# A two-layer hybrid trunk on one core: diagonal blocks through padded matrices, permuted weights in two loads

## The chip, the cores and the metric

The kernel runs on one core of one Trainium2 chip. The metric is the device time of one execution in microseconds. A core has TensorE (PE; matmuls and their weight loads), VectorE (DVE), ScalarE (ACT), GpSimd (POOL) and SyncE (SP), each with its own instruction stream. Nearly all transfers are issued by SP, in order, and carried out by 16 DMA engines.

## The reference

Two layers over 1,024 tokens of width 1,024, in float32. Layer 0 projects the input once and feeds two branches, multiplies each by its own SiLU gate, and projects both out together. Branch A is an RWKV-7 recurrence, 8 heads of 64; branch B is attention of 8 heads over a shared key and value, with the best 256 keys of each query chosen by an indexer. Layer 1 is gated linear attention. Every layer ends in a LayerNorm.

```
def step(S, inp):
    r_t, w_t, k_t, v_t, kk_t, b_t = inp
    sa = jnp.einsum('bhvk,bhk->bhv', S, -kk_t)
    S = S * w_t[:, :, None, :] + sa[..., None] * b_t[:, :, None, :] + v_t[..., None] * k_t[:, :, None, :]
    return S, jnp.einsum('bhvk,bhk->bhv', S, r_t)
...
y = jnp.concatenate([ya, yb], -1).astype(h.dtype) @ e_w_out[j]
```

## The kernel before, in words

The program runs through stages: input projections and indexer scores (to about 170 us), the rest of the projections beside the search for the 256 best keys (to 480), then one mixed stage (to about 815) in which three things run side by side, the last pieces of the output projection with the first LayerNorm (to about 900), and layer 1.

**The mixed stage** holds the attention of eight blocks of 128 queries (`attend`), the recurrence A, and pieces of the output projection. The recurrence is done in 16 chunks of 64 tokens, two chunks to a unit, eight units (`unit`, `chunk`, `finish`). For each of the 8 heads and each chunk a 64x64 triangular matrix must be inverted. `prod` computes the products and `ev_m` stores the matrices as MAB: 128 partitions (two heads' rows of 64) by 8 matrices v by 64 columns. The four 16x16 diagonal blocks of each matrix are inverted first, all 64 lanes at once:

- `f_dm` (L1167) writes the diagonal blocks from MAB to memory, d_m, with eight DMAs of 16 rows each, 8 KB a DMA, in pieces of 64 bytes.
- `f_mt` (L1173) reads them back as Mt, one block to a partition, with two DMAs of 64 rows of 1 KB.
- `f_x` and `f_sub` (L1177, L1185, L1186) run the substitution on POOL: thirty small instructions in a chain.
- `f_dt` (L1191) writes the inverses to memory, d_t, with two DMAs in pieces of 64 bytes.
- `f_tz` (L1195) clears the 128x512 tile TT on POOL, and `f_td` (L1199) reads the diagonal blocks from d_t into TT with eight DMAs.
- `z0` to `e3` (L1226 to L1286) fill in the off-diagonal blocks with small matmuls of 32x32 and 32x16, and `chunk` uses TT in `fu` (L1338).

A chunk needs the state of the chunk before it. MAB has 3 buffers, Mt and Xt 2, TT 3; d_m and d_t take turns among 3.

The order of the stage is written out by hand: each job has an engine, a cost in microseconds, its dependences and the PSUM banks it takes. A loop picks, job by job, the one that can start first by a simple clock for each engine, ties going to the longest remaining chain; for PE a bonus, MODE, favours a job of the same form as the last one (0 plain, 1 chunks and attention values, 2 and 3 the block inverse), and a change of form is charged 0.15 us. The instructions are then pinned to that order on each engine, SP's DMAs among them. So a job's stated cost alters the order of all engines.

**Weights of the output projection**, `e_w_out`, come in tiles of 128 rows by 512 columns (256 KB). For k of 4 and up the rows lie together. For k below 4 they are permuted (two heads of 64 rows each, 128 rows apart), and `rows` gives a view whose outermost size is 2. `wload` (L165), `dealt_weights` (L1555 load, L1560 ACT cast, L92 POOL difference) and `dealt_raw` (L1624) load them into wraw, of which there are three. Pieces of the projection (L1523) take their operands from yt (L1507, L1584, L1512). The attention loads qT by L896 and stores its output by L987.

Of the kernel before, what the change touches and what calls it, by code (L numbers as in the profile page):

```python
# [8 lines left out]
F32 = mybir.dt.float32  # L9
# [12 lines left out]
P = 128  # L22
# [4 lines left out]
CH = 64  # L27
# [11 lines left out]
GTA = (6, 7)  # L39
S = "s"  # L40
BANKS = ("s0", "s1", "s2", "g", "x")
MODE = 5.0
SLIP = 0.15
T0 = 2.0
PEF = 1.0
# [28 lines left out]
def trunk(ctx: ExitStack, tc: tile.TileContext, x, positions, e_w_in, a_mu, a_w0, a_w2, a_a0, a_a2,  # L74
          a_kk_scale, a_ka, a_rk, a_gn_g, a_gn_b, b_kv_norm_g, b_wuk, b_wuv, e_w_out, o_w_in, c_g2,
          c_g_bias, c_norm_g, o_w_out, ln_g, ln_b, out, dbg=None, stop=None):
    nc = tc.nc
    V, A, G, PE = nc.vector, nc.scalar, nc.gpsimd, nc.tensor
# [36 lines left out]
    ewi, ewo, owi, owo = e_w_in[0], e_w_out[0], o_w_in[0], o_w_out[0]  # L115
# [4 lines left out]
    def ct(shape, dt, name):  # L120
        return cp.tile(shape, dt, name=name)
# [40 lines left out]
    def wload(wr, w, c0, n, k, raws=3, bufs=9, scale=None, rows=None, first=None, raw=None):  # L162
        if raw is None:
            raw = (first or wr).tile([P, 512], F32, name="wraw", tag="wraw", bufs=raws)[:, :n]
            nc.sync.dma_start(raw, w[k * P:(k + 1) * P, c0:c0 + n] if rows is None else rows(k, c0, n))  # L165
        hi = wr.tile([P, 512], F32R, name="whi", tag="whi", bufs=bufs)[:, :n]
        lo = wr.tile([P, 512], F32R, name="wlo", tag="wlo", bufs=bufs)[:, :n]
        if scale is None:
            A.copy(hi, raw)  # L169
            gsub(lo, raw, f32(hi))  # L170
        else:
            A.activation(hi, raw, AF.Copy, scale=scale(k))
            V.scalar_tensor_tensor(lo, raw, scale(k), f32(hi), op0=ALU.mult, op1=ALU.subtract)
        return hi, lo
# [57 lines left out]
    d_ya = dram.tile([P, 2, 2, SEQ], F32, name="d_ya")  # L232
    d_yb = dram.tile([4, P, SEQ], F32, name="d_yb")
    d_h1 = dram.tile([SEQ, D], F32, name="d_h1")

# [57 lines left out]
    col, r0 = [], 0  # L295
# [62 lines left out]
    nc.sync.dma_start(wkv[:, 0:CH], b_wuk[0])  # L358
    nc.sync.dma_start(wkv[:, CH:], b_wuv[0])
    ixt = t1.tile([P, NT, N_IX], F32, name="ixt")  # L360
    ssq = ct([P, NT], F32, "ssq")
    sq_scr = t1.tile([P, P], F32, name="sq_scr", tag="cn", bufs=2)
    for t in range(NT):
# [662 lines left out]
    def rt(shape, name, bufs=1, dt=F32, tag=None):  # L1026
        return rw[0 if name in EARLY else 1].tile(shape, dt, name=name, tag=tag or name, bufs=bufs)

    d_m = [dram.tile([8, 8, HB, HB], F32, name=f"d_m{z}") for z in range(3)]
    d_t = [dram.tile([8, 8, HB, HB], F32, name=f"d_t{z}") for z in range(3)]  # L1030
    RUV = {}

    def ruv(c):
# [26 lines left out]
    def unit(u):  # L1060
# [102 lines left out]


        def f_dm(j):
            for g in range(8):
                nc.sync.dma_start(d_m[u % 3][:, g].rearrange("v r t -> r v t"),  # L1167
                                  U["MAB"][g * HB:g * HB + HB, :, g % 4 * HB:g % 4 * HB + HB])

        def f_mt(j):  # L1170
            U["Mt"] = rt([P, HB, HB], "Mt", 2)
            for z in range(2):
                nc.sync.dma_start(U["Mt"][RS[z]].rearrange("l p t -> l (p t)"), d_m[u % 3].rearrange("v b p t -> (v b) (p t)"))  # L1173

        def f_x(j):
            U["Xt"] = rt([P, 8, HB], "Xt", 2)
# [9 lines left out]
            G.tensor_sub(Xt[:, 0:m, jj + 1:], Xt[:, 0:m, jj + 1:], tv)  # L1186

        def f_dt(j):
            dv = d_t[u % 3].rearrange("v b (m z) t -> z (v b) m t", z=2)
            for z in range(2):  # L1190
                nc.sync.dma_start(dv[z], U["Xt"][RS[z]])  # L1191

        def f_tz(j):
            U["TT"] = rt([P, 8, CH], "TT", TB)
            G.memset(U["TT"], 0.0)  # L1195

        def f_td(j):
            for g in range(8):
                nc.sync.dma_start(U["TT"][g * HB:g * HB + HB, :, g % 4 * HB:g % 4 * HB + HB], d_t[u % 3][:, g].rearrange("v r t -> r v t"))  # L1199

        dm = job("S", 4.8, f_dm, mab)
        m_use.append(dm)
        d, use = turn("Mt", 2)
        mt = job("S", 1.2, f_mt, [dm] + d)
# [10 lines left out]
        dt_ = job("S", 1.2, f_dt, [x2_])  # L1215
        use2.append(dt_)
        d, tt_use = turn("TT", TB)
        tz = job("G", 0.6, f_tz, d)
        tt = job("S", 4.8, f_td, [dt_, tz])
        tt_use += [tz, tt]  # L1220
        U["tt_use"] = tt_use


# [261 lines left out]
    wo, operand = [[], []], {}  # L1485
    slots = [0]

    def rows(k, c0, n):

        if k >= 4:  # L1490
            return ewo[k * P:(k + 1) * P, c0:c0 + n]
        m, s = divmod(k, 2)
        return ewo[m * 256:m * 256 + 256, c0:c0 + n].rearrange("(e s d) c -> s e d c", s=2, d=CH)[s]

    def wslot(w, c0, n, k, **kw):

# [53 lines left out]
    def dealt_weights(k):  # L1550
        st = {}

        def f0(j):
            st["raw"] = w0p[0].tile([P, 512], F32, name="wraw", tag="wraw", bufs=3)
            nc.sync.dma_start(st["raw"], rows(k, 0, 512))  # L1555

        def f1(j):
            slots[0] += 1
            wo[0].append([w0p[0].tile([P, 512], F32R, name=x, tag=x, bufs=8) for x in ("whi", "wlo")])
            A.copy(wo[0][k][0], st["raw"])  # L1560

        def f2(j):
            gsub(wo[0][k][1], st["raw"], f32(wo[0][k][0]))

        d, use = turn("wraw", 3)
        a = job("S", 0.6, f0, d, late=WT[0] + WT[1] * k)
        b = job("A", 0.62, f1, [a] + ([(WOJ[-1][0],)] if WOJ else []))
        c = job("G", 1.5, f2, [b])
        use += [a, b, c]
        WOJ.append((b, c))  # L1570
# [50 lines left out]
    def dealt_raw(k):  # L1621
        def f(j):
            RAW1.append(w0p[0].tile([P, 512], F32, name="wraw", tag="wraw", bufs=3))
            nc.sync.dma_start(RAW1[k], rows(k, 512, 512))  # L1624

        d, use = turn("wraw", 3)
        use.append(job("S", 0.6, f, d, late=WT[0] + WT[1] * (NK + 1)))
# [20 lines left out]
    while left:  # L1648
        best = None
        for j in left:  # L1650
            if any(d["start"] is None for d in j["deps"] + j["behind"] + [d for d, _ in j["lag"]]):
                continue
            t = max([clock[j["e"]], j["late"]] + [d["end"] + LAT.get(d["e"], 0.0) for d in j["deps"]]
                    + [d["start"] + 0.001 for d in j["behind"]] + [d["end"] + us for d, us in j["lag"]])
            for names in j["take"]:
                t = max(t, min(held[k] for k in names))
            if t >= 1e9:
                continue
            w = tail[j["n"]] - j["plus"] + (MODE if j["e"] == "PE" and j["mode"] == mode else 0.0)
            key = (round(t / SLIP) * SLIP if j["e"] == "PE" else t, -w)  # L1660
            if best is None or key < best[0]:
                best = key, t, j
        if best is None:
            print([(j["n"], j["e"], j["f"] and j["f"].__code__.co_firstlineno, [d["n"] for d in j["deps"] if d["start"] is None]) for j in left][:60], held)
        _, t, j = best
        j["bank"] = tuple(min(names, key=lambda k: (held[k] > t, names.index(k) if held[k] <= t else held[k])) for names in j["take"])
        us = j["us"]
        if j["e"] == "PE":
            us += 0.15 * (mode != j["mode"])
            mode = j["mode"]  # L1670
        j["start"], j["end"] = t, t + us
        clock[j["e"]] = j["end"]
        for k in j["bank"]:
            held[k] = 2e9
        for g in j["gives"]:
            for k in g["bank"]:
                held[k] = j["end"] + 0.1
        left.remove(j)
        order.append(j)
# [284 lines left out]
```

## Time and profile before

| | |
|---|---|
| runs | 1350.64 us median of 3 (1349.34 to 1355.8) |
| the profiled execution | 1351.04 us, of which the span of the profile is 1349.3 us |
| granted TensorE clock, mean | 0.945 of full speed |
| busy share: PE, PE weight loads, DVE, ACT, POOL | 90%, 71%, 56%, 47%, 31% |
| DMA | 134.77 MB in 170,879 packets, 100 GB/s mean |
| the chain that ended last | PE 52%, DVE 20%, issue 9%, DMA 7%, ACT 6%, POOL 4% of the span |

The page divides the span into 40 slices and gives each engine's share in tenths; the chain that ended last is followed back from the last instruction. An engine's idle time counts only where the work that sets the end waits in it, so the stretches in which TensorE stands still are looked up one by one.

### The profile page before, as it was taken

How to read it: one execution, taken by the hardware profiler on the slowest of the kernel's cores; microseconds unless marked ns; L12 is line 12 of the kernel's file. 1: busy time of each engine (PE TensorE's matmuls, PEld its weight loads, DVE VectorE, ACT ScalarE, POOL GpSimd, SP SyncE). 2: the span in 40 equal slices, each digit the busy share in tenths (PEclk: the TensorE clock that was granted, in tenths of full speed). 3: DMA queues.
4: the chain of work that ended last, by engine and by line, in shares of the span. 5: the costliest groups of instructions: out<-in, count | busy, mean ns of one | idle time of the engine just before them, and what ended most of it. 6: DMA issues, size and time to landing. Idle time of an engine off the chain costs nothing.

```text
span 1349.3 us, 22702 instructions
## 1 busy us (share of the span) xinstructions
PE 1209.7 (90%) x8461; PEld 961.0 (71%) x8461; DVE 752.6 (56%) x1652; ACT 638.0 (47%) x1309; POOL 423.0 (31%) x725
## 2 busy tenths in 40 slices
PE   6998798999988973798999994999999999998997
PEld 5986586676766763586878773877578888887885
DVE  5146879999996542464555532684330114453666
ACT  4247768777722332676677763323651123332100
POOL 3134731444437423443434204212112331142000
PEclk9999899989989986798999996999899999999999
DMA  6102311623425364455554416863102220022321
GB/s 203 32 9 78 107 44 31 164 71 94 125 73 146 113 183 122 124 146 133 148 146 125 115 49 199 273 206 97 32 2 61 63 63 1 1 63 92 119 80 62
DMA packets 170879, 134.77 MB, mean 100 GB/s; under 512 B 62416, under 2 KB 143360, under 8 KB 170768
## 3 DMA queue, kind: packets, MB, share of 16 engines
q1 hardware_dynamic: 167680, 125.87, 32.1%
q10 hardware_dynamic: 3088, 7.44, 1.6%
q8 instruction: 67, 1.10, 0.3%
q14 instruction: 44, 0.36, 0.1%
HBM read 90.27 MB, written 42.99 MB: 99 GB/s over the span
## 4 chain that ended last, share of the span: by engine, by line
PE 52%; DVE 20%; issue 9%; DMA 7%; ACT 6%; POOL 4%; SPq 2%; DVEq 0%; POOLq 0%; ACTq 0%
DVE junk L741 7%; PE op L834 7%; PE s L1523 3%; PE dn L186 3%; PE dn L185 3%; PE dn L184 3%; PE po L979 2%; PE gt L207 2%; PE gt L206 2%; PE gt L208 2%; PE s L956 2%; DMA wraw<-in_e_w_out_dram 2%; POOL wlo L92 1%; PE dn L1860 1%; DMA yt<-d_ya 1%
## 5 line engine op out<-in xcount | busy, mean ns | idle before, releaser
L92 POOL TENSOR_TENSOR wlo<-wraw,whi 128x256 fp32r<-128x256 f32 (+1 forms) x160 | 115.7, 751 | 295.8 <-ACT whi L169 217.4
L184 PE MATMUL dn<-xh,chi 128*128 128x512 f32 x336 | 136.9, 407 | 1.3 <-DVE sg L508 0.7
L186 PE MATMUL dn<-xh,clo 128*128 128x512 f32 x336 | 136.7, 407 | 0.0
L185 PE MATMUL dn<-xl,chi 128*128 128x512 f32 x336 | 135.7, 404 | 0.0
L169 ACT CAST whi<-wraw 128x512 fp32r<-128x512 f32 (+1 forms) x72 | 43.4, 612 | 130.6 <-PE dn L185 65.8
L184 PEld LDWEIGHTS dn<-xh,chi 128*128 128x128 f32 x336 | 65.3, 194 | 22.0 <-issue 7.1
L185 PEld LDWEIGHTS dn<-xl,chi 128*128 128x128 f32 x336 | 65.4, 195 | 18.1 <-issue 4.7
L186 PEld LDWEIGHTS dn<-xh,clo 128*128 128x128 f32 x336 | 64.7, 193 | 17.9 <-issue 4.5
L92 POOL TENSOR_TENSOR clo<-craw,chi 128x256 fp32r<-128x256 f32 x84 | 75.1, 925 | 1.0
L1523 PE MATMUL s<-whi,yh 128*128 128x512 f32 x128 | 57.4, 448 | 17.7 <-DMA wraw<-in_e_w_out_dram 15.3
L424 DVE SCALAR_TENSOR_TENSOR sc<-rl,wi_s,sc 128x384 f32<-128x384 f32 (+5 forms) x42 | 45.1, 1073 | 24.2 <-ACT rl L419 21.8
L979 PE MATMUL po<-pT,v_tm 128*64 128x128 f32 x576 | 47.1, 288 | 9.6 <-DVE g L984 7.5
L92 POOL TENSOR_TENSOR vg<-vg,sg 128x256 f32<-128x256 f32 x32 | 23.7, 763 | 98.7 <-DVE vg L1886 65.1
L932 ACT ACTIVATE p<-p,mx 128x128 f32<-128x128 f32 (+7 forms) x64 | 49.6, 775 | 10.0 <-DVE mx L920 9.7
L741 DVE TENSOR_SCALAR_CACHE_REDUCE junk<-khi,Hc 128x384 bf16<-128x384 int16 (+1 forms) x64 | 51.8, 810 | 1.7
L741 DVE TENSOR_SCALAR_CACHE_REDUCE junk<-klo,Lc 128x384 bf16<-128x384 int16 (+1 forms) x64 | 51.8, 810 | 1.7
L1523 PE MATMUL s<-whi,yl 128*128 128x512 f32 x128 | 52.3, 409 | 0.0
L1523 PE MATMUL s<-wlo,yh 128*128 128x512 f32 x128 | 52.3, 409 | 0.0
L206 PE MATMUL gt<-whi,hh 128*128 128x512 f32 x128 | 51.7, 404 | 0.0
L834 PE MATMUL op<-whi,yh 128*128 128x512 f32 x128 | 51.2, 400 | 0.0
L208 PE MATMUL gt<-whi,hl 128*128 128x512 f32 x128 | 50.9, 398 | 0.0
L207 PE MATMUL gt<-wlo,hh 128*128 128x512 f32 x128 | 50.9, 398 | 0.0
(528 smaller groups left out, 3452.1 us busy)
## 6 DMA issues: line engine op xcount, KB each, us to landing
wraw<-in_o_w_in_dram SPq DMA_DIRECT2D x48, 256.0 KB
craw<-in_e_w_in_dram SPq DMA_DIRECT2D x21, 512.0 KB
xt<-in_x_dram SPq DMA_DIRECT2D x8, 512.0 KB
d_q<-qiT SPq DMA_DIRECT2D x8, 512.0 KB
d_ar<-ar SPq DMA_DIRECT2D x8, 512.0 KB
qT<-d_q SPq DMA_DIRECT2D x8, 512.0 KB
BK<-d_bk SPq DMA_DIRECT2D x8, 512.0 KB
AT<-d_ar SPq DMA_DIRECT2D x32, 128.0 KB
```

The source lines that it names most:

```text
L92: return [f(out[:, a:min(n, a + w)], *(z[:, a:min(n, a + w)] for z in ins)) for a in range(0, n, w)]
L184: PE.matmul(pst, wh[:, cs], ah[:, k, sl], start=(k == 0), stop=False)
L185: PE.matmul(pst, wh[:, cs], al[:, k, sl], start=False, stop=False)
L186: PE.matmul(pst, wl[:, cs], ah[:, k, sl], start=False, stop=(k == NK - 1))
L206: PE.matmul(pst, ah[:, k, sl], wh, start=(k == 0), stop=False)
L207: PE.matmul(pst, ah[:, k, sl], wl, start=False, stop=False)
L208: PE.matmul(pst, al[:, k, sl], wh, start=False, stop=(k == NK - 1))
L741: V.tensor_scalar(junk[:, :n], x, c[:, z:z + 1], None, op0=ALU.is_ge, op1=ALU.add, accum_out=cnt[:, z:z + 1])
L834: ins = PE.matmul(pt, a[:, k, :], b, start=(k == 0 and z == 0), stop=(k == NK - 1 and z == 2))
L932: A.activation(PB[i, h][:, :n], PB[i, h][:, :n], AF.Exp, scale=-1.0, bias=m[:, h, k - 1:k], accum_out=rsum[:, h:h + 1])
L979: PE.matmul(po[RS[s], g * P:(g + 1) * P], v_tm[:, kt, :], pT[:, (2 * z + s) * P:(2 * z + s + 1) * P], start=(kt == 0 and g == 0), stop=(kt ...
L1523: PE.matmul(pt, a[:, k, :], b, start=(k == 0 and z == 0), stop=(k == NK - 1 and z == 2))
```

## The change

d_m and d_t become padded matrices in memory: each of 64 blocks has a stride DG of 16 x 64 + 16 floats. With it, a whole 64x64 matrix is stored by rows, and the diagonal block of each lane starts at a multiple of DG; `half_rows` is the view by rows of a half of the partitions, `blocks` the view by diagonal blocks. f_dm and f_td use two DMAs each for eight, and carry the off-diagonal columns along in rows of 256 bytes. f_mt and f_dt use `blocks`, so Mt is read in pieces of 64 bytes. The off-diagonal zeros of TT come from d_t, which is cleared once early on; f_tz is gone. The permuted weights load by two DMAs of 64 rows each. The costs that the planner is told, its bonus and its charge for a change of form are altered.

```diff
-MODE = 5.0
+MODE = 3.0
+CHANGE = (0.22, 0.13, 0.1, 0.1)
...
-            nc.sync.dma_start(raw, w[k * P:(k + 1) * P, c0:c0 + n] if rows is None else rows(k, c0, n))
+            if rows is None:
+                nc.sync.dma_start(raw, w[k * P:(k + 1) * P, c0:c0 + n])
+            else:
+                rows(raw, k, c0, n)
...
+    DG = 16 * CH + 16
+    d_m = [dram.tile([64 * DG], F32, name=f"d_m{z}") for z in range(3)]
+    d_t = [dram.tile([64 * DG], F32, name=f"d_t{z}") for z in range(3)]
...
+    nil = t1.tile([CH, DG], F32, name="nil")
+    V.memset(nil, 0.0)
+    for z in range(3):
+        nc.sync.dma_start(d_t[z].rearrange("(p c) -> p c", p=CH), nil)
...
-    d_m = [dram.tile([8, 8, HB, HB], F32, name=f"d_m{z}") for z in range(3)]
-    d_t = [dram.tile([8, 8, HB, HB], F32, name=f"d_t{z}") for z in range(3)]
+    def half_rows(d, z):
+
+        return d.rearrange("(v x) -> v x", x=8 * DG)[:, z * 4 * DG:z * 4 * DG + CH * CH].rearrange("v (p c) -> p v c", c=CH)
+
+    def blocks(d):
+
+        return d.rearrange("(l x) -> l x", x=DG)[:, :HB * CH].rearrange("l (r c) -> l r c", c=CH)[:, :, 0:HB]
...
         def f_dm(j):
-            for g in range(8):
-                nc.sync.dma_start(d_m[u % 3][:, g].rearrange("v r t -> r v t"),
-                                  U["MAB"][g * HB:g * HB + HB, :, g % 4 * HB:g % 4 * HB + HB])
+            for z in range(2):
+                nc.sync.dma_start(half_rows(d_m[u % 3], z), U["MAB"][RS[z]])
 
         def f_mt(j):
             U["Mt"] = rt([P, HB, HB], "Mt", 2)
             for z in range(2):
-                nc.sync.dma_start(U["Mt"][RS[z]].rearrange("l p t -> l (p t)"), d_m[u % 3].rearrange("v b p t -> (v b) (p t)"))
+                nc.sync.dma_start(U["Mt"][RS[z]], blocks(d_m[u % 3]))
...
-            dv = d_t[u % 3].rearrange("v b (m z) t -> z (v b) m t", z=2)
+            dv = blocks(d_t[u % 3]).rearrange("l (m z) t -> z l m t", z=2)
...
-        def f_tz(j):
+        def f_td(j):
             U["TT"] = rt([P, 8, CH], "TT", TB)
-            G.memset(U["TT"], 0.0)
-
-        def f_td(j):
-            for g in range(8):
-                nc.sync.dma_start(U["TT"][g * HB:g * HB + HB, :, g % 4 * HB:g % 4 * HB + HB], d_t[u % 3][:, g].rearrange("v r t -> r v t"))
-
-        dm = job("S", 4.8, f_dm, mab)
+            for z in range(2):
+                nc.sync.dma_start(U["TT"][RS[z]], half_rows(d_t[u % 3], z))
+
+        dm = job("S", 1.2, f_dm, mab)
...
-        tz = job("G", 0.6, f_tz, d)
-        tt = job("S", 4.8, f_td, [dt_, tz])
-        tt_use += [tz, tt]
+        tt = job("S", 1.2, f_td, [dt_] + d)
+        tt_use += [tt]
...
-    def rows(k, c0, n):
+    def rows(raw, k, c0, n):
 
         if k >= 4:
-            return ewo[k * P:(k + 1) * P, c0:c0 + n]
+            nc.sync.dma_start(raw, ewo[k * P:(k + 1) * P, c0:c0 + n])
+            return
         m, s = divmod(k, 2)
-        return ewo[m * 256:m * 256 + 256, c0:c0 + n].rearrange("(e s d) c -> s e d c", s=2, d=CH)[s]
+        for e in range(2):
+            r0 = m * 256 + e * P + s * CH
+            nc.sync.dma_start(raw[RS[e]], ewo[r0:r0 + CH, c0:c0 + n])
...
-            us += 0.15 * (mode != j["mode"])
+            us += (mode != j["mode"]) * CHANGE[j["mode"]]
```

## Rows read from the trace of the kernel before

**Rows 1.** Busy us of each engine by stretch (x instructions), then granted clock, DMA share, GB/s

```profile
507.00:551.00 44.00, 16.01 (x96) 13.12 (x98) 11.07 (x33) 15.43 (x42) 17.32 (x60) 0.67 0.46 133
551.00:561.00 10.00, 10.00 (x177) 7.08 (x174) 3.03 (x8) 3.89 (x10) 5.92 (x15) 0.58 0.46 125
561.00:812.00 251.00, 237.45 (x3992) 191.95 (x3990) 132.57 (x341) 177.49 (x380) 79.90 (x241) 0.98 0.44 121
812.00:829.00 17.00, 1.06 (x5) 0.83 (x6) 3.02 (x5) 4.74 (x10) 5.58 (x8) 0.60 0.58 186
829.00:873.00 44.00, 41.55 (x171) 33.16 (x171) 24.61 (x48) 15.80 (x27) 19.92 (x25) 0.92 0.82 259
```

**Rows 2.** Timeline of PE: start, us, instruction, idle before it and its releaser

```profile
517.21 2.04 PE L1111 MATMUL x<-AT,BK 128*128 128x128 f32 x8 [7.47 <-DMA BK<-d_bk]
...
531.77 0.66 PE L914 MATMUL s<-KH,qT 128*128 128x384 f32 x1 [10.81 <-DMA qT<-d_q]
...
550.60 1.55 PE L979 MATMUL po<-pT,v_tm 128*64 128x128 f32 x12 [7.48 <-DVE g L984]
...
828.59 0.80 PE L1523 MATMUL s<-whi,yh 128*128 128x512 f32 x1 [15.27 <-DMA wraw<-in_e_w_out_dram]
```

**Rows 3.** Timeline of SP's queue: start, us of issuing, line, DMA

```profile
503.61 4.14 SPq L1167 DMA_DIRECT2D d_m<-MAB  x8
...
512.89 0.56 SPq L1067 DMA_DIRECT2D BK<-d_bk  x1
...
517.95 4.55 SPq L896 DMA_DIRECT2D qT<-d_q  x1
522.55 0.63 SPq L1555 DMA_DIRECT2D wraw<-in_e_w_out_dram  x1
...
531.48 6.37 SPq L1191 DMA_DIRECT2D d_t<-Xt  x2
...
544.87 3.65 SPq L1199 DMA_DIRECT2D TT<-d_t  x8
```

**Rows 4.** Timeline of ACT: casts of the permuted weights

```profile
530.66 0.62 ACT L1560 CAST whi<-wraw 128x512 fp32r<-128x512 f32 x1 [5.20 <-DMA wraw<-in_e_w_out_dram]
536.73 0.62 ACT L1560 CAST whi<-wraw 128x512 fp32r<-128x512 f32 x1 [5.45 <-DMA wraw<-in_e_w_out_dram]
```

**Rows 5.** Chain that ended last, in order of time: start, us, transfers of 256 KB

```profile
817.61 9.75 DMA wraw<-in_e_w_out_dram
...
855.31 4.90 DMA yt<-d_ya
...
1236.95 3.28 DMA wraw<-in_o_w_out_dram
```

**Rows 6.** Timeline of POOL: first substitution, and a weight split among it

```profile
510.65 0.22 POOL L1185 TENSOR_TENSOR itmp<-Mt,Xt 128x15 f32<-128x15 f32 x1 [20.54 <-DMA Mt<-d_m]
...
525.54 1.41 POOL L92 TENSOR_TENSOR wlo<-wraw,whi 128x256 fp32r<-128x256 f32 x2 [6.15 <-ACT whi L1560]
```

**Rows 7.** Instructions by tile (d_m, d_t, TT): count, ns min/median/max, first and last start

```profile
L1167 SPq DMA_DIRECT2D d_m<-MAB x64: 303/429/1261, 495.4 to 727.7; - x64
L1173 SPq DMA_DIRECT2D Mt<-d_m x16: 473/596/2061, 507.8 to 733.1; - x16
...
L1199 SPq DMA_DIRECT2D TT<-d_t x64: 303/430/1648, 544.9 to 758.5; - x64
L1191 SPq DMA_DIRECT2D d_t<-Xt x16: 513/626/4009, 531.5 to 748.8; - x16
...
L1195 POOL MEMSET TT<- x8: 518/525/531, 487.0 to 709.0; 128x512 f32 x8
```

**Rows 8.** Waits of SP's queue from 560 to 815 us: total, times, longest

```profile
SPq L1199 <- DMA d_t<-Xt: 6.8, 3, 3.5
```

**Rows 9.** Timeline of PE: a matmul after another form, and the next

```profile
800.91 0.50 PE L1523 MATMUL s<-whi,yh 128*128 128x512 f32 x1
801.25 0.40 PE L1523 MATMUL s<-wlo,yh 128*128 128x512 f32 x1
```

More of the change, by code (lines that the diff above doesn't have):

```diff
@@ L1554, in f0 @@
             st["raw"] = w0p[0].tile([P, 512], F32, name="wraw", tag="wraw", bufs=3)
-            nc.sync.dma_start(st["raw"], rows(k, 0, 512))
+            rows(st["raw"], k, 0, 512)
         def f1(j):
@@ L1623, in f @@
             RAW1.append(w0p[0].tile([P, 512], F32, name="wraw", tag="wraw", bufs=3))
-            nc.sync.dma_start(RAW1[k], rows(k, 512, 512))
+            rows(RAW1[k], k, 512, 512)
         d, use = turn("wraw", 3)
```

## The prediction

> **What bounds the kernel now.** I read the share of each engine first: TensorE is busy for 90% of the span, so time is mostly lost where it stands still. The table by stretch shows where that is [rows 1]: from 507 to 551 us it is busy 16.0 of 44 us, at a granted clock of 0.67 of full speed (a mean over its two levels, 1.2 and 2.4 GHz); from 551 to 561 it is busy throughout, but at 0.58, so mostly on the lower level after the standstill; from 812 to 829 it works 1.1 of 17 us. Between them, 561 to 812, it is busy 237.5 of 251 us, so there the work itself sets the time. The DMA engines are only 0.46 busy in the first hole: bandwidth as a whole is not what is short.
>
> Then I asked what ended each of TensorE's idle times [rows 2]: BK's load (7.5 us), qT's load (10.8), an attention output whose bank the vector engine gave back late (7.5), and at the end the load of wraw (15.3). The queue of SP tells why these are late [rows 3]. From 503.6 SP issues without a pause: eight DMAs for d_m take 4.1 us, BK's load comes out only at 512.9, and then the issue of one qT load takes 4.55 us at 518.0, of two d_t stores 6.4 us at 531.5. An issue normally takes 0.3 to 0.65 us, so something ahead is full.
>
> What stands ahead are the loads of permuted output weights (k below 4), 256 KB each. ACT's casts wait for them [rows 4]: two casts start at 530.66 and 536.73, 6.1 us apart, each ended by its load, so 256 KB per 6.1 us, 43 GB/s; the load issued at 522.55 [rows 3] lands 14.2 us later. At the end the same kind of load takes 9.75 us, while 256 KB in whole rows take 3.3 us where little else moves and a yt read of 256 KB takes 4.9 us in the most crowded stretch [rows 5]; the table has 259 GB/s there [rows 1]. One shape moves at a sixth of what the engines move together.
>
> The permuted view's outermost size is 2, and I conclude that it occupies 2 of 16 DMA engines. The Trainium skill ("DMA: Bandwidth & Descriptors", section "Why a DMA increments its semaphore by 16 and not by 1") says that a transfer uses the largest number of engines up to 16 that divides both sides' slowest size, here 2; the 43 GB/s agree.
>
> Behind ACT's casts POOL is stuck as well [rows 6]: its substitution for the first unit begins at 510.65, after 20.5 us of waiting for Mt, and is then held behind a weight split that waits 6.2 us for ACT. Its blocks come back as TT only from 544.87 on [rows 3], and the recurrence of sixteen chunks can't start before.
>
> **The change, part by part.** (a) Permuted weights, two DMAs of 64 rows each. Seven loads are planned jobs or stand right in front of pieces (k 0 to 3 of the first half, 0 to 2 of the second), the eighth is that of 817.6. Each adds an issue; the nearest SP rows are 0.60 to 0.63 us [rows 7], so 8 x 0.6 = 5 us more on SP in all. A landing falls from 9.75 to 14.2 us to between 3.3 and 4.9 [rows 5]; I take 4.9 in the crowd.
>
> (b) d_m and TT go from eight DMAs each to two. By the medians [rows 7] a unit had 8 x 0.429 + 8 x 0.430 = 6.9 us of issue; the new four cost 4 x 0.63 = 2.5 us by the d_t row, which is nearest since its view also has many small pieces. That is 4.4 us a unit and 35 us of SP over eight units, nearly all of it while TensorE is busy anyway. On the path it counts in the first hole: the eight issues at 503.61 stand right ahead of BK.
>
> (c) Landings. The off-diagonal parts travel too, so d_m and TT move 128 KB instead of 32 KB per half, in rows of 256 bytes instead of 64; Mt reads the blocks in 64-byte pieces, 1,024 to a DMA instead of 64 rows of 1 KB. No row has that Mt read. From below: as before, 0. From above: d_t's stores, with half as many pieces, made SP wait up to 3.5 us for their landing [rows 8], so at most 3.5 us more. I take 1 us, since the three waits of that group together are 6.8 us, 2.3 on average, and a fixed part is in them. For seven units this lies beside TensorE's work at 95% busy; if that cover goes, it is 1 to 3.5 us a unit.
>
> (d) POOL loses eight memsets of 0.525 us [rows 7], 4.2 us, off the path: 0.
>
> (e) Once at the start: a memset of 64x1040 on the vector engine, about twice the length of the 128x512 one just named, so about 1.1 us as an estimate, and three stores of 266 KB. They need no result and nobody waits for them before d_t's first use, hundreds of us later. Cover gone, if they were queued ahead of the first loads: 0.8 MB at the 133 GB/s of the hole [rows 1] is 6 us. I take 0; range 0 to 6.
>
> (f) The planner: the four costs of SP jobs fall, the bonus for staying in a matmul form falls from 5 to 3, and a change of form is charged 0.22, 0.13, 0.1 or 0.1 instead of 0.15. So every engine's order is written anew. What a change of form costs shows in a matmul that follows another form, 0.50 against 0.40 us [rows 9]: 0.1 us. By the code there are 32 block-inverse jobs, 48 of the chunks and 80 of the attention values that are not in the plain form, at most 320 changes. If a fifth of these came or went, that is 6 us either way; I take 0.
>
> **The sum.** First hole: of 28.0 us idle [rows 1], BK's wait keeps about 4 (its issue moves up by some 2.8 us of d_m's and the rest is landing), qT's about 4 (issued some 4 us earlier and landing in 4 to 5 rather than behind 2 full engines), the late bank 0: the chain there is a yt load behind permuted weights and ACT. So 20 us back. Clock: the 551 to 561 stretch gives back up to 10 x 0.42 = 4.2 us, if TensorE hasn't stood still before; I take 4. At the end: 9.75 to 4.9, 5 us; what follows, 829 to 873, is full of transfers at 0.82 [rows 1] and merely moves forward. Sum 29 us; Mt's extra 1 us lies in the first hole, covered by the earlier start of the substitution. The profiled execution took 1351.0 us (span 1349.3), 0.4 above the median of the runs; 1351.0 - 29 = 1322.
>
> Bounds: the first hole from 12 us (only qT's wait) to 32 (all idle time, and the clock); the end from 0 to 10; order 6 either way; start 0 to 6.
>
> **The rivals.** One: halves don't help. The Trainium skill, same page, section "Rules for kernel authors", advises against two transfers to disjoint partition halves, since they serialise on the same engines and one of 128 partitions does as well. As a mechanism here, the permuted loads are slow for what stands beside them and not for their shape: then only (b) is left, some 3 us ahead of BK, and what an earlier qT and TT win, about 5: 1351 - 8 = 1343. Against it speaks that the DMA engines were half idle while the load took 14.2 us, and that the yt read took 4.9 us in more traffic [rows 1, 5]. By that rule the gain is 8, by the rows 29. Chance 0.09.
>
> Two: the new order gives it back. The 561 to 812 stretch has only 13.5 us of idle time [rows 1]; if the planner puts attention matmuls where the chunks' chain should go, or changes form 100 times more and loses some of that overlap, 25 us are gone: about 1347, same. Nothing in the profile of before can show the new order; all its forms stay. Chance 0.08, 0.03 of it beyond 0.5% on the slow side.
>
> Three, the slow one: the block gather becomes the wait. Mt stands between d_m and POOL's thirty instructions of every unit. If pieces of 64 bytes land late by more than about 8 us a unit, TensorE waits for TT in each: with 29 us won elsewhere, it decides from 29/8 = 3.6 us exposed per unit. At 5 us exposed: 1322 + 40 = 1362. For it: twice d_t's pieces. Against it: units are prepared ahead, and d_t's 3.5 us at the longest held up SP rather than TensorE. Chance 0.05.
>
> Four: the recurrence starts so much earlier, at about 520 rather than 550, that even the stretch to 812 loses its gaps: 13.5 us idle, of which perhaps 8, and the rest of the first hole: 1322 - 16 = 1306. Chance 0.06.
>
> **How the numbers follow.** The forecast has the remaining 0.72. A measurement of this kernel can tell about 0.5%, 7 us, from no change. Faster by more: forecast 0.72, rival four 0.06, two thirds of rival one 0.06, together 0.84. Same: rest of rival one 0.03, of rival two 0.05, 0.08. Slower: rival three 0.05 and 0.03 of rival two, 0.08. The range reaches down past rival four, to 1303, and up to rival one, 1343: that leaves out rivals two and three and a little on each side, under 2 in 10.
>
> **What would show it.** In the changed profile: DMAs for d_m and TT 16 each, not 64; permuted wraw landing within 5 us, and no SP issue over 2 us between 515 and 540; TensorE's wait for qT under 5 us and the one at the attention bank gone; the granted clock of that stretch over 0.9; the end's wait near 10 us rather than 15.3. I am wrong on (a) if permuted loads still come 6 us apart; on (c) if POOL's substitution waits for Mt in units after the second; on (f) if the busy time of TensorE grows by over 6 us.

## The result, and the profile after

The changed kernel takes 1340.59 us (median of 5 runs, 1337.82 to 1342.63) against 1353.73 for the kernel before in the same measurement: a ratio of 0.9907, with a 95% interval of 0.9882 to 0.9932. It is faster by 13 us, inside the range, but by less than half of the 29 us that were forecast. Two repeats gave 0.9898 and 0.9867 (below). The profiled execution took 1337.82 us.

The page's span and engine shares, and then the table by stretch, with the columns of [rows 1]:

```profile
span 1336.1 us, 22563 instructions
...
PE 1206.5 (90%) x8461; PEld 958.1 (72%) x8461; DVE 753.0 (56%) x1653; ACT 635.7 (48%) x1309; POOL 414.3 (31%) x717
```

```profile
507.00:538.00 31.00, 20.16 (x256) 15.88 (x256) 13.56 (x42) 18.38 (x52) 17.80 (x61) 0.83 0.74 192
538.00:561.00 23.00, 23.00 (x486) 17.94 (x484) 10.96 (x28) 15.92 (x40) 8.97 (x22) 0.93 0.61 163
561.00:700.00 139.00, 124.90 (x2121) 103.50 (x2116) 73.98 (x195) 93.55 (x208) 56.67 (x190) 0.95 0.61 156
700.00:799.00 99.00, 94.30 (x1420) 74.65 (x1419) 51.11 (x123) 69.45 (x142) 12.43 (x38) 1.00 0.30 85
799.00:813.00 14.00, 1.76 (x20) 1.10 (x18) 3.08 (x4) 4.47 (x10) 7.68 (x10) 0.68 0.65 199
489.20:798.40 309.20, 277.42 (x4388) 225.59 (x4388) 156.92 (x419) 206.32 (x466) 96.79 (x313) 0.95 0.53 139
```

The same view of the kernel before, over four stretches that the rows ahead of the prediction don't have: two pieces of the first hole, the stretch from 561 to 700, and the whole mixed stage:

```profile
526.00:528.40 2.40, 0.00 (x0) 0.00 (x0) 0.76 (x2) 0.00 (x0) 1.33 (x4) 0.50 0.13 51
532.50:535.90 3.40, 3.40 (x13) 3.06 (x14) 2.82 (x11) 0.00 (x0) 0.67 (x3) 0.54 0.13 51
...
561.00:700.00 139.00, 130.57 (x2233) 106.20 (x2232) 76.62 (x207) 97.47 (x217) 55.22 (x167) 0.96 0.51 138
...
487.10:812.70 325.60, 282.09 (x4407) 228.54 (x4407) 157.30 (x421) 208.28 (x466) 105.92 (x323) 0.92 0.45 124
```

The last line of each table is the mixed stage, from TensorE's first products for the recurrence to the last transposes of the recurrence's output. It fell from 325.6 to 309.2 us, 16.4 us. TensorE's busy time in it fell by 282.1 - 277.4 = 4.7 us (at a clock of 0.95 for 0.92) and its idle time from 43.5 to 31.8. Ahead of the stage the profiled execution is 2.1 us later (489.2 for 487.1) and behind it 1.1 us longer (1336.1 - 798.4 = 537.7 for 536.6), so 16.4 - 3.2 = 13.2 us, as measured. A single profile moves by some microseconds ahead of the stage (it starts at 487 to 491 us in the seven profiles without the clearing of d_t, at 488 to 496 in the eleven with it), so from here on profiles are compared from the start of the stage.

The first hole has shrunk about as foretold: 10.8 us idle from 507 to 538 and none from 538 to 561, where there were 28.0 from 507 to 551 and the sum left 8. But from 561 to 700 TensorE now stands idle for 14.1 us where it was 8.4: something of the gain is given back. What TensorE waits for from 480 to 880 us, by its view of waits (total, times, longest):

```profile
PE s L1540 <- DMA wraw<-in_e_w_out_dram: 12.8, 1, 12.8
PE s L927 <- DMA qT<-d_q: 6.6, 2, 5.0
PE x L1130 <- DMA BK<-d_bk: 5.7, 1, 5.7
PE g L927 <- ACT pT L974: 3.4, 1, 3.4
PE s L1249 <- DVE Tn L1240: 2.9, 1, 2.9
PE x L1249 <- DVE rsum L954: 2.9, 1, 2.9
```

Against [rows 2]: the wait for the attention bank (7.48) is gone, qT's longest is 5.0 for 10.8, BK keeps 5.7 of 7.5, and the wait at the end 12.8 of 15.3. New is the block inverse (L1249), with two waits of 2.9 us: one at 535.7 us, behind the attention's rsum, and one behind 561 us, for its own chain on the vector engine (Tn). SP's queue in the first hole, and the instructions by tile:

```profile
508.57 1.30 SPq L1186 DMA_DIRECT2D d_m<-MAB  x2
509.92 1.43 SPq L1510 DMA_DIRECT2D wraw<-in_e_w_out_dram  x2
511.45 0.53 SPq L909 DMA_DIRECT2D qT<-d_q  x1
...
512.78 2.23 SPq L1191 DMA_DIRECT2D Mt<-d_m  x2
515.05 4.53 SPq L1104 DMA_DIRECT2D AT<-d_ar  x2
519.63 0.61 SPq L1086 DMA_DIRECT2D BK<-d_bk  x1
...
527.67 1.27 SPq L1214 DMA_DIRECT2D TT<-d_t  x2
```

```profile
L1186 SPq DMA_DIRECT2D d_m<-MAB x16: 595/602/1490, 497.5 to 709.4; - x16
L1191 SPq DMA_DIRECT2D Mt<-d_m x16: 584/608/2417, 502.5 to 714.6; - x16
...
L1214 SPq DMA_DIRECT2D TT<-d_t x16: 590/618/687, 527.7 to 732.5; - x16
```

d_m and TT have 16 DMAs each, at the 0.6 us that were costed, and the first unit's blocks come back from 527.7 instead of 544.9 [rows 3]. SP still loses time at one place: two AT loads take 4.53 us to issue, behind permuted loads, a qT load and the block gather, and hold BK's load up behind them.

### The profile page after: what moved, and what is told of

It is laid out like the page before. It is cut to its first block, busy times and chain, and to the rows that moved or that the text cites. A ratio compares the mean times of both kernels' runs of the same rounds, so it can differ in the third digit from the quotient of the medians.

```text
span 1336.1 us, 22563 instructions
## 1 busy us (share of the span) xinstructions
PE 1206.5 (90%) x8461; PEld 958.1 (72%) x8461; DVE 753.0 (56%) x1653; ACT 635.7 (48%) x1309; POOL 414.3 (31%) x717
## 4 chain that ended last, share of the span: by engine, by line
PE 49%; DVE 19%; issue 10%; DMA 9%; ACT 7%; POOL 4%; SPq 2%; DVEq 0%; POOLq 0%; ACTq 0%
DVE junk L754 7%; PE op L847 7%; PE dn L190 3%; PE dn L189 3%; PE dn L188 3%; PE s L1540 3%; PE po L992 2%; PE gt L211 2%; PE gt L210 2%; PE gt L212 2%; PE s L969 2%; DMA wraw<-in_e_w_in_dram 2%; DMA yt<-d_yb 2%; PE dn L1877 1%; PE s L927 1%
## 5 line engine op out<-in xcount | busy, mean ns | idle before, releaser
L188 PEld LDWEIGHTS dn<-xh,chi 128*128 128x128 f32 x336 | 65.4, 195 | 21.9 <-issue 6.8
L1540 PE MATMUL s<-whi,yh 128*128 128x512 f32 x128 | 56.8, 444 | 14.7 <-DMA wraw<-in_e_w_out_dram 12.8
L847 PE MATMUL op<-wlo,yh 128*128 128x512 f32 x128 | 50.7, 396 | 0.0
```

What stands on the lines that cost most here:

```text
L188: PE.matmul(pst, wh[:, cs], ah[:, k, sl], start=(k == 0), stop=False)
L847: ins = PE.matmul(pt, a[:, k, :], b, start=(k == 0 and z == 0), stop=(k == NK - 1 and z == 2))
L1540: PE.matmul(pt, a[:, k, :], b, start=(k == 0 and z == 0), stop=(k == NK - 1 and z == 2))
```

## The experiments

Sixteen runs, each beside the kernel before on the same chip. What each edit leaves of the plan matters: without the planner's new numbers the planned order of the mixed stage is that of before.

**Halves alone.** The kernel before, with the permuted loads in two DMAs.

```diff
-        return ewo[m * 256:m * 256 + 256, c0:c0 + n].rearrange("(e s d) c -> s e d c", s=2, d=CH)[s]
+        for e in range(2):
+            r0 = m * 256 + e * P + s * CH
+            nc.sync.dma_start(raw[RS[e]], ewo[r0:r0 + CH, c0:c0 + n])
```

> The kernel before with the permuted weights loaded by two DMAs of 64 rows and nothing else; the order of the mixed stage is that of before. Theory A (these loads filled two DMA engines and held up all that came behind them; the changed kernel's new order then gave part of the gain back): 10 to 18 us faster than before, about 1338, with the idle time of 507 to 551 us falling from 28 to some 12 us. Rival B (the halves do nothing, the gain of 13 us came from fewer issues for d_m and TT): within 3 us of before. Rival C (the halves are the whole of the gain and the rest is worth nothing): 13 us faster, the same as the changed kernel.

1333.78 against 1349.52 us, 0.9871 [0.9847, 0.9894], and 0.986 in a second measurement of the same kernel (below). This part alone gives at least what the whole change gives. The table by stretch of its profile, over a piece of the first hole, from 561 to 700 and over the stage, and then its waits:

```profile
523.00:530.00 7.00, 3.23 (x17) 2.96 (x15) 2.79 (x6) 1.97 (x4) 3.26 (x10) 0.50 0.93 260
...
561.00:700.00 139.00, 132.63 (x2428) 108.82 (x2429) 79.59 (x215) 101.01 (x224) 55.25 (x171) 1.00 0.56 151
...
490.70:794.40 303.70, 274.53 (x4406) 223.86 (x4406) 157.15 (x421) 208.35 (x466) 105.21 (x323) 0.96 0.49 132
```

```profile
PE s L1529 <- ACT yh L1518: 13.5, 3, 12.7
PE s L917 <- DMA qT<-d_q: 9.2, 2, 5.4
PE x L1114 <- POOL itmp L1188: 8.7, 1, 8.7
...
PE po L982 <- DVE g L987: 2.3, 1, 2.3
```

Where the permuted loads queued, the DMA engines are now 0.93 busy at 260 GB/s. In the kernel before, the two pieces of the hole shown above have 0.13 at 51 GB/s, and 2 of 16 engines would be 0.125. The stage is 21.9 us shorter: 7.6 us less busy (at a clock of 0.96 for 0.92) and 14.3 less idle. BK's wait has not become shorter: 8.7 us at the matmul that reads AT and BK. The row puts it down to POOL's itmp, but BK's load went out only 5.1 us before that matmul, at 517.33, and I read the wait as BK's. In the kernel before, BK's load goes out ahead of the first permuted load (512.89, 516.12), so the halves have nothing to move out of its way. qT's wait and the bank's have become shorter.

**The same number of DMAs, but cut by columns.** The kernel before, each permuted tile in two DMAs of 256 columns, whose views keep the outermost size of 2.

```diff
+        for c in range(0, n, 256):
+            nc.sync.dma_start(raw[:, c:c + 256],
+                              ewo[m * 256:m * 256 + 256, c0 + c:c0 + c + 256].rearrange("(e s d) c -> s e d c", s=2, d=CH)[s])
```

> The kernel before with each permuted weight tile loaded by two DMAs of 256 columns, so that there are two DMAs as in the change but the outermost size of the view stays 2. If the shape was the trouble (2 of 16 DMA engines): no gain, within 5 us of before or slower, the casts still some 6 us apart. If two smaller DMAs are what helps: 10 to 18 us faster, like the halves.

1358.95 against 1351.72, 1.0058 [1.0033, 1.0084]: slower. Its stretch from 538.4, and its casts of these weights:

```profile
538.40:541.00 2.60, 1.57 (x25) 1.14 (x20) 0.00 (x0) 1.92 (x6) 1.22 (x2) 1.00 0.13 49
```

```profile
526.22 0.62 ACT L1566 CAST whi<-wraw 128x512 fp32r<-128x512 f32 x1 [2.40 <-DMA wraw<-in_e_w_out_dram]
532.39 0.62 ACT L1566 CAST whi<-wraw 128x512 fp32r<-128x512 f32 x1 [5.55 <-DMA wraw<-in_e_w_out_dram]
539.08 0.62 ACT L1566 CAST whi<-wraw 128x512 fp32r<-128x512 f32 x1 [6.07 <-DMA wraw<-in_e_w_out_dram]
```

6.2 and 6.7 us apart, as in [rows 4], and again 0.13 of the engines, though several of these DMAs are in flight. So it is the shape that counts, and not the number: with DMAs on different pairs of engines the share would be above 0.13. That is what the Trainium skill ("DMA: Bandwidth & Descriptors", "Why a DMA increments its semaphore by 16 and not by 1") would have: the slowest sizes of both sides set how many engines take part, and for DMAs issued from SP they are the lowest-numbered ones each time. The Trainium skill's advice on the same page ("Rules for kernel authors") against two transfers to disjoint halves does not hold for a view like this one (0.9871 and 0.986 with halves), since it takes for granted that the one transfer would use all engines.

**Padded matrices alone.** The kernel before with the padded d_m and d_t and their four DMAs a unit, the planner's costs and charges as before.

```diff
-            for g in range(8):
-                nc.sync.dma_start(d_m[u % 3][:, g].rearrange("v r t -> r v t"),
-                                  U["MAB"][g * HB:g * HB + HB, :, g % 4 * HB:g % 4 * HB + HB])
+            for z in range(2):
+                nc.sync.dma_start(half_rows(d_m[u % 3], z), U["MAB"][RS[z]])
```

> The kernel before with the padded matrices (two DMAs each for d_m and TT, Mt by 64-byte pieces, cleared d_t) and nothing else; the planner is told the old costs, so the order of the mixed stage is that of before. Theory A: 3 to 8 us faster (BK's load some 3 us earlier, SP less crowded). Rival B: 8 to 13 us faster. Rival C: within 3 us of before; if the block gather is a new wait, slower.

1352.32 against 1349.52, 1.0014 [0.9995, 1.0033]: nothing. Its waits are nearly those of [rows 2], BK's and the bank's unchanged, qT's longest 8.9 for 10.8:

```profile
PE s L1534 <- ACT yh L1523: 16.0, 4, 15.1
PE s L923 <- DMA qT<-d_q: 13.5, 2, 8.9
PE x L1126 <- DMA BK<-d_bk: 7.6, 1, 7.6
PE po L988 <- DVE g L993: 7.5, 1, 7.5
```

The issue time saved is real, and it is spent again. From ACT's last store into MAB to POOL's first substitution, the mean of units 3 to 8 is 13.8 us before and 13.6 here. Taken apart: d_m's issue falls from 4.9 to 1.9 us, but Mt's begins 6.4 us behind it instead of 4.1, and from the end of Mt's issue to POOL's first use of it there are 3.3 us instead of 2.4. The last 0.9 us I take for what the gather of 64-byte pieces costs (0.6 between halves alone and both transfers). In this profile the stage is 320.6 us, 5.0 shorter than before, but it starts 3.3 later and 2.3 more follow it; the runs show no gain.

**Both transfers, old order.** The whole change, with the costs, the bonus and the charge of before.

```diff
...
-        dm = job("S", 1.2, f_dm, mab)
+        dm = job("S", 4.8, f_dm, mab)
...
+        tz = job("G", 0.6, None, d)
+        tt = job("S", 4.8, f_td, [dt_, tz])
...
-            us += (mode != j["mode"]) * CHANGE[j["mode"]]
+            us += 0.15 * (mode != j["mode"])
```

> Both changes of the transfers, the old planner: the order of the mixed stage is that of before. Theory A: 18 to 25 us faster than before and so 5 to 12 us faster than the changed kernel, since the new order gave that back. Rival C: like the changed kernel, 13 us faster, the order being worth nothing. Rival D (the new order wins and the transfers are worth less than foreseen): less than 10 us faster.

1334.0 against 1349.52, 0.9879 [0.9857, 0.9902], as halves alone. The padded matrices add nothing to the halves either. So theory A is out, by which they win 3 to 8 us and the new order gives 5 to 12 back; it is rival C, the halves are the whole of the gain.

**The order alone.** The transfers of before, with the new costs, bonus and charges, TT's clearing at the head of the job that loads it.

```diff
-MODE = 5.0
+MODE = 3.0
+CHANGE = (0.22, 0.13, 0.1, 0.1)
...
-        dm = job("S", 4.8, f_dm, mab)
+        dm = job("S", 1.2, f_dm, mab)
```

> The transfers of before (eight DMAs each for d_m and TT, permuted weights in one DMA) in the changed kernel's order: bonus 3, the new charges for a change of form, SP costs of 1.2. The memset of TT sits at the head of its load's job. Theory A: 3 to 12 us slower than before. Rival C: within 3 us. Rival D: 3 to 10 us faster.

1371.12 against 1349.52, 1.0149 [1.0125, 1.0174]: with the old transfers this order costs 22 us, more than any of the theories had. Whether it is that the plan takes SP for quicker than it is, or the bonus, the charges or the clearing in TT's job, this run does not tell.

**The change without halves.** All of the change but the permuted loads, which are one DMA again (the first diff backwards).

```diff
-        for e in range(2):
-            r0 = m * 256 + e * P + s * CH
-            nc.sync.dma_start(raw[RS[e]], ewo[r0:r0 + CH, c0:c0 + n])
+        return ewo[m * 256:m * 256 + 256, c0:c0 + n].rearrange("(e s d) c -> s e d c", s=2, d=CH)[s]
```

> The changed kernel with the permuted weights in one DMA each again. Theory A2: the halves are the gain, so 12 to 25 us slower than the changed kernel, 1.002 to 1.01 of before. Rival F (in the new order the halves matter less, the padded matrices carry the gain): within 5 us of the changed kernel.

1357.91 against 1350.77, 1.0057 [1.0036, 1.0078]. Together with the repeat of the whole change on that chip, the halves are worth 1357.91 - 1337.58 = 20.3 us within it.

**Which halves.** First only the load behind the mixed stage, then only the four loads of the first half of the columns (rows2 is the version with two DMAs).

```diff
-        wo[1].append(wslot(ewo, 512, 512, k, rows=rows, raw=RAW1[k] if k < 3 else None) if k < 4 else
+        wo[1].append(wslot(ewo, 512, 512, k, rows=rows2, raw=RAW1[k] if k < 3 else None) if k < 4 else
```

> The kernel before with the halves only for the one permuted load behind the mixed stage (the 9.75 us at 817.6); all planned loads stay in one DMA. By the forecast's term for the end: 5 us faster. If the end is held by the other transfers there, 0 to 2 us.

1354.01 against 1351.72, 1.0019 [1.0003, 1.0036]: nothing, where I had 5 us. The chain that ended last, of this kernel, and its TensorE at that place:

```profile
821.99 7.68 DMA yt<-d_yb
```

```profile
826.89 0.79 PE L1536 MATMUL s<-whi,yh 128*128 128x512 f32 x1 [12.31 <-ACT yh L1525]
```

The load went out at 818.86 and its cast began at 822.21, 3.4 us for 9.75 [rows 5]. But the read of yt issued behind it at 820.24 is there only for a cast (yh) at 826.22, 6.0 us later, and that cast ends TensorE's wait instead: 12.31 us for 15.27. The next read of yt, the one in the chain, takes 7.7 us. From TensorE's first matmul after the wait to the end of the span it is 1350.0 - 826.9 = 523.1 us, where it was 1349.3 - 828.6 = 520.7: what the wait gave up is paid behind it.

```diff
-            nc.sync.dma_start(st["raw"], rows(k, 0, 512))
+            rows2(st["raw"], k, 0, 512)
```

> The kernel before with the halves only for the four loads of the first half (516 to 530 us); those of the second half (570 to 590, and the last) stay in one DMA. If the first hole is the whole gain: 13 to 17 us faster, as with all eight. If the three loads of 570 to 590 were a second hole, as the recurrence's fifth chunk suggests, some 6 us less: 8 to 12 us faster.

1337.91 against 1351.72, 0.9905 [0.9883, 0.9928]: 13 to 14 us of the 16 to 21 that all halves give, at the edge between my two cases. With the last load at nothing, the rest, some 5 us by the ratios (0.9905 for 0.9871 and 0.986, with intervals that just touch), falls to the three loads of the second half, issued around 570 to 592 us, which I had counted only for their extra issues. SP's queue there before, and with halves alone:

```profile
575.40 6.18 SPq L1167 DMA_DIRECT2D d_m<-MAB  x8
...
592.31 3.72 SPq L1077 DMA_DIRECT2D RUV<-d_vt  x2
...
599.25 6.48 SPq L1167 DMA_DIRECT2D d_m<-MAB  x8
```

```profile
573.60 1.76 SPq L1499 DMA_DIRECT2D wraw<-in_e_w_out_dram  x2
...
578.13 1.99 SPq L1499 DMA_DIRECT2D wraw<-in_e_w_out_dram  x2
580.28 1.19 SPq L1080 DMA_DIRECT2D RUV<-d_vt  x2
...
585.54 4.31 SPq L1170 DMA_DIRECT2D d_m<-MAB  x8
```

Before, two loads of RUV take 3.72 us and d_m's eight 6.48 behind the permuted loads of 588.10 and 590.31; with all halves 1.19 and 4.31, and with the first four halves alone, where these loads are whole, still 3.33 and 7.11. They feed the recurrence. The eight of the third unit, shown first, gain little (5.82 us with halves).

**The order, with the new transfers.** The whole change repeated twice, and five variants of the planner's numbers. MODE 5 and the old charge of 0.15, with the new costs:

```diff
-MODE = 3.0
-CHANGE = (0.22, 0.13, 0.1, 0.1)
+MODE = 5.0
...
-            us += (mode != j["mode"]) * CHANGE[j["mode"]]
+            us += 0.15 * (mode != j["mode"])
```

> The changed kernel as it is, on the same chip as the three that follow. All theories: 0.988 to 0.993 of before. Theory A2 (the halves win some 16 us, the padded matrices nothing, and the new order gives 3 to 7 us back): above both transfers in the old order, which was 0.988. Rival E (the order is neutral): also 0.988.

> The changed kernel with the old bonus of 5 and the old charge of 0.15 for every change of form; SP costs of 1.2 and no memset job, so that only the costs of the planner are new. Theory A2, if the lower SP costs spoil the order: 0.991 or more, like the changed kernel or slower. If the bonus and the charges spoil it: 0.988 or less. Rival E: 0.988 to 0.991.

The whole change again 1337.58 against 1350.77, 0.9898 [0.9876, 0.992]; with the old bonus and charge 1334.06, 0.9873 [0.985, 0.9896]. The old costs of SP with the new bonus and charges:

```diff
-        dm = job("S", 1.2, f_dm, mab)
+        dm = job("S", 4.8, f_dm, mab)
...
-        tt = job("S", 1.2, f_td, [dt_] + d)
+        tt = job("S", 4.8, f_td, [dt_, tz])
```

> The changed kernel with the old SP costs of 4.8 and an empty memset job in the planner, so that only the bonus and the charges are new. Theory A2, if the bonus and the charges spoil the order: 0.991 or more. If the SP costs do: 0.988 or less. Rival E: 0.988 to 0.991.

1343.31, 0.9952 [0.9934, 0.9971]. The old bonus and charge again, and the seven permuted loads told as the two issues that they are:

```diff
-        a = job("S", 0.6, f0, d, late=WT[0] + WT[1] * k)
+        a = job("S", 1.2 if k < 4 else 0.6, f0, d, late=WT[0] + WT[1] * k)
...
-        use.append(job("S", 0.6, f, d, late=WT[0] + WT[1] * (NK + 1)))
+        use.append(job("S", 1.2, f, d, late=WT[0] + WT[1] * (NK + 1)))
```

> The changed kernel with the old bonus and charge, and the planner told 1.2 us for the seven planned permuted loads, which now take two issues each. If what the planner is told of SP still matters: 2 to 6 us faster than without it (0.987 of before), so below both kernels. If SP is no longer short: no difference.

1338.81 against 1351.72, 0.9922 [0.9897, 0.9947]: telling the planner the truth did not help; it comes out above the 0.9873 without it, which neither of my cases had. Last, on one chip, halves alone again, the whole change again, and the change with only the flat charge or only the old bonus:

```diff
-CHANGE = (0.22, 0.13, 0.1, 0.1)
+CHANGE = (0.15, 0.15, 0.15, 0.15)
```

```diff
-MODE = 3.0
+MODE = 5.0
```

> The halves alone in the kernel before, again, beside the changed kernel on one chip. If the new order gives something back: 0.986 to 0.988, and 2 to 6 us below the changed kernel. If order and padded matrices are worth nothing: equal to it within 2 us.

> The changed kernel as it is, for comparison on the same chip: 0.989 to 0.991 by every theory.

> The changed kernel with the bonus of 3 and the old charge of 0.15 for every change of form. If the bonus is what costs: 0.99 or more. If the charges are: 0.987 or 0.988. If it is chance how an order falls out: anything from 0.985 to 0.996.

> The changed kernel with the old bonus of 5 and the new charges. If the charges are what costs: 0.99 or more. If the bonus is: 0.987 or 0.988. If it is chance: anything from 0.985 to 0.996.

Against 1352.58: halves alone 1331.75, 0.986 [0.9839, 0.9881]; the whole change 1335.09, 0.9867 [0.9845, 0.9889], below the 0.989 to 0.991 that I expected by every theory; flat charge 1330.37, 0.9847 [0.9826, 0.9869]; old bonus 1334.32, 0.9869 [0.984, 0.9897]. The intervals overlap, so none of the four is shown to beat another; all beat the kernel before. Orders between 0.985 and 0.995 came out of small changes to the planner's numbers, and no run says what makes one of them good.

## Why the prediction was right or wrong

The table follows the recurrence, from the first matmul rows of the chunks in TensorE's timeline, in microseconds after the start of the stage in that profile.

| profile | second chunk starts | sixth chunk starts | last transposes |
|---|---|---|---|
| before | 88.3 | 158.1 | 325.6 |
| halves alone | 72.5 | 136.3 | 303.7 |
| first four halves | 71.5 | 139.9 | 309.1 |
| the change | 65.9 | 121.9 | 309.2 |
| the change, flat charge | 63.7 | 126.2 | 304.3 |

**The cause was right.** The permuted loads are slow for their shape and hold up what queues behind them; the run with halves alone, and the one with the number of DMAs alone, show it. Rival One (halves don't help) is out: 0.9871 and 0.986.

**The first hole's 20 us of idle time and 4 of clock** were right for the hole and wrong for the end. In the terms of the sum, for the changed kernel: the hole gave 17.2 us for 20 (28.0 to 10.8), and TensorE's busy time in the stage fell by 4.7 for the 4 of clock. From 561 to 700, which the sum had at nothing, 5.7 us of idle time came back (8.4 to 14.1). The rest of the stage adds 0.2, and that makes its 16.4. Behind the stage 1.1 us were lost where 5 were forecast, and ahead of it 2.1: 13.2 in all, for 29.

So two steps failed. One is silent: that what the hole gives back reaches the end of the stage whole. The other is the end's 5 us, below. The first shows in what TensorE waits for from 561 to 700 in the changed kernel:

```profile
PE g L927 <- ACT pT L974: 3.4, 1, 3.4
PE s L1249 <- DVE Tn L1240: 2.9, 1, 2.9
PE cb L1358 <- issue: 2.7, 1, 2.7
PE x L1249 <- DVE Tn L1240: 1.8, 1, 1.8
PE s L1294 <- ACT Gs L1286: 1.7, 1, 1.7
```

L1249 and L1294 are the block inverse: 6.4 us, where the kernel before waits 0.2 us and halves alone do not wait at all. Both repeats of the change have it too (7.2 and 7.1 us), so it belongs to the new order. No one number of the planner makes it: among the five variants it lies between 0 (flat charge; old costs) and 4.3 us, and the slowest of them, with the old costs, has none and stands idle elsewhere. Which of the order's choices costs the time stays open.

With the order of before, the second chunk starts 88.3 - 72.5 = 15.8 us sooner: less than 24, because BK's wait stayed at 8.7 where I had left it 4 (by my own figures 7.5 - 2.8 = 4.7, and the 2.8 come from (b), which is not in this kernel), and the bank kept 2.3 where I had 0 (qT, 3.8, was as I took it). These 15.8 are kept to the end. In the changed kernel it starts 22.4 us sooner, near the 24, and the sixth chunk even 36.2. But at the end of the stage 16.4 are left: TensorE has some 275 to 282 us of work in the stage, whichever chain is ahead, so a lead of the recurrence is not yet time won. This is rival Two in part, 5.5 us less at the end of the stage than halves alone, and half of rival Four: the recurrence did start earlier, block inverses at 535.7 for 554.2, but the idle time behind 561 grew. Of my signs three failed: the clock of the hole (0.83 from 507 to 538, for over 0.9), the longest issue (4.53 us, for 2) and the wait at the end (12.8 us, for near 10).

**The end's 5 us** were wrong. The load fell by 6.4 us, more than I took, and the wait by 3.0; but the first matmul needs a read of yt as well, and what comes next needs more of them. In three profiles of the changed kernel 534.8 to 537.7 us follow the stage, before it was 536.6. In the profile of halves alone the chain that ended last passes through the same read:

```profile
802.50 8.39 DMA yt<-d_yb
```

I wrote that what follows is full of transfers and "merely moves forward". It does not move forward: the load that lands sooner gives its place in the chain to a read of yt, and the time stays.

**The three loads near 570 to 592** were wrong in the other direction. I counted them in part (a) for their issues and nowhere for their landing, since TensorE was 95% busy there. They are worth some 5 us: with the old order the sixth chunk starts 21.8 us sooner for 15.8 at the second, 6.0 more, and with the first four halves alone 18.2 for 16.8, 1.4 more. That SP's queue is what holds the recurrence there is likely but not isolated: with the padded matrices alone, which also shorten SP's issues, the sixth chunk comes 63.9 us after the second (halves alone 63.8, before 69.8), and yet the runs show no gain.

**The padded matrices** ((b), (c) and (d)) were right where I put them off the path, and even the 3 us ahead of BK did not show: with them alone, from d_m's first issue to BK's there are 8.3 us for 9.3, and BK's wait is 7.6 for 7.5. The issues cost 0.60 to 0.62 us as foretold. The 1 us for the gather is near the 0.9 measured; with the shorter issue of d_m and the later one of Mt it makes 13.6 for 13.8 us from MAB to the substitution. Rival Three is out. Its sign, a wait of POOL for Mt in later units, was badly chosen: POOL waits for Mt seven times in both kernels, 38.0 us in all before and 44.3 after, and in the units after the second TensorE is busy through all of them in the changed kernel. The long issues in the changed kernel, 2.23 us for the Mt pair and 4.53 for the AT pair behind it, are not the gather's by itself: with the padded matrices in the old order, with halves or without, the same pairs took 1.30 and 1.33. They come with the new order, in which other loads stand ahead.

**The clearing of d_t** costs 1.83 us of SP. I took 0 for the rest, and that is not certain: TensorE is busy for 145.3 us of the first 170 where it was 146.9, and the stage starts at 491.2 us on average in the eleven profiles with the clearing and at 488.7 in the seven without. The ranges overlap, and no run has the clearing alone.

```profile
34.52 1.83 SPq L373 DMA_DIRECT2D d_t<-nil  x3
```

**The order, 0 with 6 either way,** is what the runs leave open. The two measurements of halves alone and that of both transfers with the old order average 0.9870, the three of the change 0.9891, with intervals of 0.002 either way; on the one chip where both were timed side by side, 1331.75 and 1335.09 overlap. So the new order gains nothing over the old one, and may give back some 3 us; the variants show that orders can give back 10. With the old transfers it cost 22.

So the sum for halves alone is 15.8 (for 24) + 6.0 (for 0) + 0 (for 5) = 21.8 us of the stage; its profile starts the stage 3.6 us later and ends 1.3 later behind it, and the spans differ by 17.0, near the 16 to 21 us of its two measurements. That is 22 us in the stage, where 24 were forecast, and nothing of the 5 behind it. The changed kernel reaches less of it, 16.4.

## What to carry to other kernels

Look at the DMA share of a short stretch in which only transfers of one shape move: 0.13 means two engines of sixteen, and the outermost size of the view is the place to look. Cut such a transfer so that the outermost size of each piece is large (64 here, and the share became 0.93), not merely into more pieces, and expect the gain where something short stands behind it in the queue, also in stretches where TensorE seems busy. Time won for a chain in the middle of a stage is only worth what the other work of the stage leaves of it, so a forecast should follow it to the end of the stage.

## What had not been expected of the hardware

DMAs of 256 KB that together run on two engines at 51 GB/s do not only land late: the issue of quite other DMAs behind them took up to 4.55 us for one and 6.37 for two [rows 3], while in two pieces of that stretch the other fourteen engines had nothing to do. Why SP's queue stands still then, no run shows. The gather of 1,024 pieces of 64 bytes to a DMA was ready for use only 0.6 to 0.9 us later than 64 rows of 1 KB. And with each of these loads cut into two DMAs by columns, with several in flight, no more moved than before, 49 GB/s.
